# Hybrid retention and sliding-window layer: one chain of retention steps for all heads, the second value pair moved to the front, and a bias table stored from 128 partitions

## The chip, the cores and the metric

The kernel runs on one core of a Trainium2 chip. The core has a matrix engine (TensorE; PE in the profile), a vector engine (VectorE, DVE), a scalar engine (ScalarE, ACT), a general engine (GpSimd, POOL) and SyncE (SP), which here only issues transfers between the on-chip memory and HBM. Each engine works through its own instructions strictly in order. The metric is device time in microseconds (us); lower is better.

## The reference

One step of a one-layer encoder for 1024 prompt tokens and 64 sample tokens (1088 columns in all, T in the code), model width 1024:

```python
rq, rk, rv, rg, sq, sk, sv, ga, gb = split(rms_norm(x, g_attn) @ w_in)
q, k = rope(rq), rope(rk) / 16                      # 4 heads of width 256; v = rv
s = (q @ k.T) * decay ; o = s @ v + (q @ state) * q_dec       # per chunk and head
state = state * gamma**C + (k * k_dec).T @ v                  # handed to the next chunk
a = (rms_norm(o) * silu(rg)) @ w_ret_out
b = attend(sq, band(sk), band(sv), bias_table, sinks) @ w_swa_out   # 16 heads of width 64
x = x + (sigmoid(ga) * a + sigmoid(gb) * b) @ w_mix_out
x = x + cross_attention(rms_norm(x), memory)
x = x + (silu(rms_norm(x) @ w_gate) * (rms_norm(x) @ w_up)) @ w_down
y = rms_norm(x)
```

The 64 sample tokens start from a given retention state and given caches. Outputs are y, the retention states, the last keys and values of the window, and the keys and values of the memory.

## The kernel before

Every fp32 operand of the large products is split into a high and a low part (`split`: a cast on ScalarE, the rest on VectorE, L125 and L126), and each product is made of three matmuls (high·high, high·low, low·high). The stage that the change touches is the first, `project_phase` (L612), which takes about the first 700 us.

**Pairs and products.** The columns of `w_in` are taken in pairs of 128-column tiles (256 columns). A pair is one 2x2 Strassen multiplication (`strassen`, L265): seven products named P1 to P7, each of 24 matmuls on TensorE (L209, L210, L212; four blocks of six). For a pair the weights are loaded (`raw`), summed on GpSimd (L186 to L193) and split into `wq`. The right-hand operands B11 to B22 and T1 to T4 are made once from x at the start (`start_phase`). A product lies in one of three PSUM bank pairs (`pq`) until VectorE or ScalarE has read it (L270, L644).

**What follows a pair.** `rotated` (keys and queries, L663) applies the rotary angles with eight VectorE products and four sums for each pair; the sums are on VectorE for heads 0 and 1 and on GpSimd for heads 2 and 3. `values` (L687) only stores. `queries` (L693) orders the window queries and stores them from GpSimd's queue into `d_sq`. Keys, queries and values of the retention go to a scratch tensor in HBM, `d_qkv`. `stage` is the ring of eight buffers that all of these write.

**The first pair** (values of head 0) is done plainly with eight products (`plain`, L233), while the Strassen operands are still being made. The weights of the second pair are prepared inside `start_phase` on VectorE.

**Retention as side steps.** The retention of a head (`retention`, L827) is a Python generator. It loads four blocks of 256 tokens in turn and the 64 sample tokens last. Each `yield` ends a step: after every Strassen product one step is emitted into TensorE's order (`product`, L215), so that its VectorE and ScalarE work has the next product to hide behind. A block has five steps: transposes of keys and values (`pk`, L823), an empty one, scores (`pss`), the state's update with the transposes of the block's earlier output (`pkv`, `pb` L982), output (`po`). The sample tokens add four (`pk`, `psss`, `pb`, then `pos` and `pkvs`), with the first load one, so 25 steps for a head. `finish_side` (L775) emits whatever steps are left without products between them.

**Sum of squares.** `token_squares` (L505) adds up x squared for the norm, with 14 sums on VectorE (L516); `token_roots` (L518) reduces them over the partitions on TensorE (`pt`, L525) and takes the roots, and `spread_roots` (L530) spreads them again (`pb`, L536). Retention needs them.

**Bias table.** `bias_table` (L584) makes the relative-position bias with one matmul, 16 heads by 256 distances, copies it to `rb` and stores it 64 times over into `d_rb` (1 MB) with one transfer from GpSimd's queue (L597). `bias_rows` (L606) reads it back skewed into `d_bias`.

**Order.** Pairs run k0, q0, k1, q1, v1, window queries 0, k2, q2, v2, window queries 1, k3, q3, v3, window queries 2, window keys/values, window queries 3, gates. Between them a list scheduler, led by priorities and its own timing model, decides the order within each engine; TensorE's order of products and steps is fixed by the code (`in_order`, L1024).

Of the kernel before, what the change touches and what calls it, by code (L numbers as in the profile page):

```python
# [11 lines left out]
F32 = mybir.dt.float32  # L12
# [7 lines left out]
P = 128  # L20
# [7 lines left out]
BLK = 256  # L28
NBLK = SEQ // BLK
H = 4  # L30
# [80 lines left out]
class Kernel:  # L111
# [310 lines left out]
    def start_phase(self, ctx):  # L422

        nc, tc, io = self.nc, self.tc, self.io
# [53 lines left out]
                if k == 2 and n < 2:  # L478
                    weight(1, n)
        with tc.issue_after(behind[0]), tc.issue_after(behind[1]):  # L480
            self.second = self.weight_ops(self.load_raws([io["w_k"][i] for i in range(2)]), by=nc.vector)
            for k in range(4):
                b11, b12 = qs[k][:2]
                for b in (b11, b12):
                    nc.scalar.mul(b, b, g[:, k:k + 1])
                nc.vector.tensor_tensor(out=b12, in0=b12, in1=b11, op=ALU.subtract)
# [97 lines left out]
    def bias_table(self):  # L584

        nc, io = self.nc, self.io
        t = self.ra.tile([P, BLK + 16], F32, tag="sf", bufs=1, name="table")
        rb = self.ra.tile([P, 2, BLK], F32, tag="ot", bufs=1, name="rb")[:16]
        table, onehot = t[:32, BLK:], t[:32, :BLK]
        self.load(table, io["rel_bias"])  # L590
        self.load(onehot, io["c_onehot"])
        pb = self.norm_psum("pb")
        nc.tensor.matmul(pb[:16, :256], table, onehot, start=True, stop=True)
        for i in range(2):
            nc.vector.tensor_copy(rb[:, i, :], pb[:16, :256])
        rb = rb.rearrange("h i c -> h (i c)")
        nc.gpsimd.dma_start(self.d_rb.rearrange("h (i c) -> h i c", c=512), rb.unsqueeze(1).broadcast_to([16, 32, 512]))  # L597
        row = self.np.tile([1, 16], F32, tag="row", bufs=1, name="row")
        self.load(row, io["sinks"])
        ps = self.norm_psum("ps")  # L600
        nc.tensor.matmul(ps[:, :16], self.ones[:1, :], row, start=True, stop=True)
        for e in range(2):
            rows = slice(e * 64, (e + 1) * 64)
            nc.vector.tensor_copy(self.sinks[rows, :], ps[rows, :16].rearrange("p (a b) -> p a b", b=2)[:, :, e])
# [7 lines left out]
    def project_phase(self):  # L612
        nc, tc, io = self.nc, self.tc, self.io
        with ExitStack() as ctx:
# [5 lines left out]
            first = self.start_phase(sctx)  # L620
# [66 lines left out]
            def values(w, h, by=self.strassen):  # L687
                def emit(i, t, ps, sb):
                    self.store(self.d_qkv[2, 2 * h + i, :, half(t)], taken(ps, sb))
                by(w, self.ops, emit)  # L690

            pair = lambda w, h: self.load_ops([io[w][2 * h + i] for i in range(2)])
# [30 lines left out]
            first = self.second  # L723
            sctx.close()
            stage, long, count = *self.stage_tiles(), [0]
            with ExitStack() as rctx:
                self.ra = rctx.enter_context(tc.tile_pool(name="ra", bufs=1, reuse_waits="tile"))
                rope = self.ra.tile([P, 2, T], F32, name="rope")
                self.load(rope, io["c_rope"])
                self.out = None  # L730
                rotated(first, 0, 1)
                with tc.issue_after(self.sums_done):
                    self.token_squares()
                self.side = self.retention_begin()
                rotated(pair("w_q", 0), 0, 0)
                for h in range(1, H):
                    rotated(pair("w_k", h), h, 1)
                    if h == 1:
                        self.finish_side()
                        self.side = self.retention_steps(0)  # L740
                    rotated(pair("w_q", h), h, 0)
                    values(pair("w_v", h), h)
                    queries(pair("w_sq", h - 1), h - 1)
                    self.finish_side()
                    self.side = self.retention_steps(h)
                project(self.load_ops((io["w_sk"], io["w_sv"])), lambda i, t, o: nc.gpsimd.dma_start(self.d_skv[i, :, half(t)], o))
                with tc.issue_after(self.last_sum):
                    self.bias_rows()
                queries(pair("w_sq", 3), 3)
                for m in (0, 2, 4):  # L750
                    gate_columns(1, "w_ga", AF.Sigmoid, m)
                self.finish_side()
# [24 lines left out]
            pass  # L777
        self.side = None

    def retention_begin(self):  # L780
        for i in range(6):
            yield
        self.token_roots()
        self.retention_setup()
        for i in range(3):
            yield
        self.spread_roots()
        yield

    def retention_steps(self, h):  # L790
        yield from self.retention(h)
        if h == 1:
            yield
            self.bias_table()
        if h == H - 1:
            for i in range(3):
                yield
            self.ret_turn(*self.out)

    def retention_setup(self):  # L800

# [1077 lines left out]
```

## Time and profile before

| | |
|---|---|
| median of 3 runs | 2258.58 us (2257.07 to 2261.13) |
| the profiled execution | 2261.93 us, span 2260.1 us |
| TensorE busy | 2171.1 us, 96% of the span |
| VectorE, ScalarE, GpSimd busy | 1596.2, 879.3, 702.6 us |
| granted TensorE clock, mean | 0.984 |

In a row of a timeline the columns are start (us from the span's start), duration, engine, source line, operation, output<-input by the names in the program, shape, and in brackets the engine's idle time just ahead of the row and what ended it. A row of a window table gives the stretch, its length, the busy time of each engine with the number of instructions in brackets, the granted TensorE clock, the busy share of the transfer engines, and GB/s. In a table of waits stand the waiting engine and line, what it waited for, the sum in us, the number of times and the longest. Transfers have sizes in KB and the median time from issue to landing.

### The profile page before, as it was taken

The numbers are of one execution on the slowest core, as the hardware profiler recorded it, in microseconds if no ns is written. First come the engines' busy times: TensorE is split into PE (matmuls) and PEld (weight loads), VectorE is DVE, ScalarE is ACT, GpSimd is POOL, SyncE is SP. The second block draws the span as 40 slices with busy tenths as digits, with TensorE's granted clock in tenths as the row PEclk, the third lists the DMA queues.
The fourth block names the chain that finished last, engine by engine and source line by source line (L and its number), as shares of the span: only waits on it lengthen the run. The fifth ranks groups of instructions, "written<-read, shape, count | busy, mean of one in ns | idle before, by whom it ended". The sixth has DMA issues, their size and how long they took to land.

```text
span 2260.1 us, 42145 instructions
## 1 busy us (share of the span) xinstructions
PE 2171.1 (96%) x16620; PEld 2117.7 (94%) x16620; DVE 1596.2 (71%) x2696; ACT 879.3 (39%) x1895; POOL 702.6 (31%) x522
## 2 busy tenths in 40 slices
PE   9699998999999998999999999999999999999987
PEld 8698998999999996888999999999999999999987
DVE  7886676867668657876544556668777776879787
ACT  6334332435444346554233334333322322335333
POOL 0123234354246111230000000004555555534571
PEclk9799999999999999999999999999999999999999
DMA  5334344443444557325543212332333223376332
GB/s 210 124 104 137 102 129 100 128 133 112 164 140 154 163 202 240 123 77 183 149 141 104 82 39 66 120 105 83 101 131 122 93 101 116 113 246 209 120 120 80
DMA packets 160455, 291.90 MB, mean 129 GB/s; under 512 B 21538, under 2 KB 89058, under 8 KB 160130
## 3 DMA queue, kind: packets, MB, share of 16 engines
q1 hardware_dynamic: 151122, 263.97, 36.0%
q0 software_dynamic: 5104, 17.44, 2.5%
q10 hardware_dynamic: 4032, 7.80, 0.9%
q8 instruction: 131, 2.15, 0.4%
q14 instruction: 66, 0.54, 0.1%
HBM read 197.99 MB, written 91.95 MB: 128 GB/s over the span
## 4 chain that ended last, share of the span: by engine, by line
PE 73%; DVE 12%; DMA 5%; issue 4%; ACT 3%; POOL 3%; SPq 0%; POOLq 0%; DVEq 0%; ACTq 0%
PE pq L209 14%; PE pq L212 14%; PE pq L210 14%; PE pd L152 7%; PE pd L153 7%; PE pd L154 7%; DVE wq L126 2%; DMA hl<-d_op 1%; DVE T L126 1%; PE pss L1103 1%; DVE B L126 1%; PE pout L1169 1%; DVE stage L644 1%; DVE u L270 1%; PE pp L1146 1%
## 5 line engine op out<-in xcount | busy, mean ns | idle before, releaser
L126 DVE TENSOR_TENSOR wq<-raw,wq 128x512 fp32r<-128x512 f32 (+1 forms) x505 | 460.1, 916 | 164.3 <-ACT wq L125 162.2
L125 ACT CAST wq<-raw 128x512 fp32r<-128x512 f32 (+1 forms) x505 | 305.6, 613 | 608.2 <-PE pq L212 255.7
L209 PE MATMUL pq<-T,wq 128*128 128x272 f32 x1832 | 505.5, 294 | 15.5 <-DVE stage L644 5.7
L210 PE MATMUL pq<-T,wq 128*128 128x272 f32 x1832 | 500.0, 289 | 0.6 <-DVE T L126 0.6
L209 PE MATMUL pq<-B,wq 128*128 128x272 f32 x1526 | 419.9, 293 | 0.7 <-DVE stage L644 0.6
L210 PE MATMUL pq<-B,wq 128*128 128x272 f32 x1526 | 415.7, 289 | 0.6 <-DVE B L126 0.5
L212 PE MATMUL pq<-T,wq 128*128 128x272 f32 x1832 | 380.7, 289 | 2.4 <-DVE wq L126 2.4
L186 POOL TENSOR_TENSOR raw<-raw 128x512 f32<-128x512 f32 (+1 forms) x58 | 78.7, 1357 | 962.5 <-DVE rs_r L309 486.0
L209 PEld LDWEIGHTS pq<-T,wq 128*128 128x128 f32 x1832 | 347.7, 190 | 18.6 <-issue 6.9
L210 PEld LDWEIGHTS pq<-T,wq 128*128 128x128 f32 x1832 | 351.3, 192 | 1.1 <-DVE T L126 1.1
L212 PE MATMUL pq<-B,wq 128*128 128x272 f32 x1526 | 317.0, 288 | 0.0
L210 PEld LDWEIGHTS pq<-B,wq 128*128 128x128 f32 x1526 | 291.9, 191 | 1.0 <-DVE B L126 1.0
L209 PEld LDWEIGHTS pq<-B,wq 128*128 128x128 f32 x1526 | 289.0, 189 | 1.8 <-DVE stage L644 0.9
L212 PEld LDWEIGHTS pq<-T,wq 128*128 128x128 f32 x1832 | 286.3, 189 | 2.7 <-DVE wq L126 2.6
L212 PEld LDWEIGHTS pq<-B,wq 128*128 128x128 f32 x1526 | 238.2, 189 | 0.0
L270 DVE TENSOR_TENSOR u<-pq,u 128x544 f32<-128x544 f32 x177 | 127.1, 718 | 87.0 <-PE pq L212 86.5
L189 POOL TENSOR_TENSOR raw<-raw 128x512 f32<-128x512 f32 (+1 forms) x58 | 82.7, 1426 | 122.1 <-DVE wq L126 122.1
L644 DVE TENSOR_TENSOR stage<-pq,u 128x544 f32<-128x544 f32 x112 | 80.1, 716 | 42.5 <-PE pq L212 31.0
L193 POOL TENSOR_TENSOR raw<-raw 128x512 f32<-128x512 f32 (+1 forms) x58 | 88.5, 1527 | 15.7 <-DVE wq L126 12.2
L1131 POOL TENSOR_TENSOR t<-t,den 128x768 f32<-128x768 f32 (+2 forms) x34 | 47.7, 1402 | 137.7 <-DVE nm L1119 53.0
L187 POOL TENSOR_TENSOR raw<-raw 128x512 f32<-128x512 f32 (+1 forms) x58 | 85.3, 1471 | 3.7
L1661 POOL TENSOR_TENSOR y<-u,y 128x544 f32<-128x544 f32 x38 | 61.4, 1632 | 49.6 <-DVE y L1659 29.2
(403 smaller groups left out, 4748.7 us busy)
## 6 DMA issues: line engine op xcount, KB each, us to landing
hl<-d_op SPq DMA_DIRECT2D x84, 272.0 KB, 4.0
d_op<-stage SPq DMA_DIRECT2D x44, 272.0 KB, 2.2
d_op<-ht SPq DMA_DIRECT2D x44, 272.0 KB, 3.9
raw<-w_gate SPq DMA_DIRECT2D x22, 512.0 KB, 3.6
raw<-w_up SPq DMA_DIRECT2D x22, 512.0 KB, 4.6
raw<-w_down SPq DMA_DIRECT2D x16, 512.0 KB, 3.8
d_qkv<-stage SPq DMA_DIRECT2D x28, 272.0 KB, 2.5
d_gate<-stage ACTq DMA_DIRECT2D x28, 272.0 KB, 2.1
```

The lines of the kernel that those rows point to most:

```text
L125: self.last_cast = self.nc.scalar.copy(hi, src).ins
L126: self.last_low = self.nc.vector.tensor_tensor(out=lo, in0=src, in1=hi.bitcast(F32), op=ALU.subtract).ins
L152: mm(ps, wh, xh, start=start, stop=False)
L153: mm(ps, wh, xl, start=False, stop=False)
L154: self.last_mm = mm(ps, wl, xh, start=False, stop=stop).ins
L187: tt(out=a21, in0=a21, in1=a22, op=add)
L193: self.last_sum = tt(out=a12, in0=a12, in1=a11, op=sub).ins
L209: mm(ps[:, c, :HC], w[:, 0, ks], x[:, 0, cs], start=start, stop=False)
L210: mm(ps[:, c, :HC], w[:, 0, ks], x[:, 1, cs], start=False, stop=False)
L212: self.last_mm = mm(ps[:, c, :HC], w[:, 1, ks], x[:, 0, c * HC:(c + 1) * HC], start=False, stop=stop).ins
L270: add = lambda out, a, b: nc.vector.tensor_tensor(out=out, in0=a, in1=b, op=ALU.add)
L644: nc.vector.tensor_tensor(out=o, in0=ps, in1=sb, op=ALU.add)
```

## The change

Four things are done.

1. The second pair, prepared in `start_phase`, is the values of head 1 instead of the keys of head 0. The keys of head 0 become the third pair, with weights prepared by GpSimd as for the others. Values of head 1 no longer stand between q1 and window queries 0.
2. The four generators of the heads, and the one for the roots ahead of them, become a single one, `retention_steps`. It starts after q0 (before: the roots with q0, head 0 with q1), and it is finished once, after the third gate pair. No head's remaining steps are emitted at the end of a pair group. In all 112 products carry its steps.
3. Within the chain the roots are three steps in, the spreading three steps later, and the bias table stands right behind head 1.
4. The bias matmul's weights are widened by a VectorE copy from 16 columns to 128, each head eight times over. The result lies on 128 partitions, and each stores four of the 32 repetitions that before 16 partitions stored.

```diff
@@ start_phase
-            self.second = self.weight_ops(self.load_raws([io["w_k"][i] for i in range(2)]), by=nc.vector)
+            self.second = self.weight_ops(self.load_raws([io["w_v"][2 + i] for i in range(2)]), by=nc.vector)
@@ bias_table
-        rb = self.ra.tile([P, 2, BLK], F32, tag="ot", bufs=1, name="rb")[:16]
+        rb = self.ra.tile([P, 2, BLK], F32, tag="ot", bufs=1, name="rb")
+        wide = self.ra.tile([P, P], F32, tag="qsm", bufs=1, name="wide")[:32]
...
-        nc.tensor.matmul(pb[:16, :256], table, onehot, start=True, stop=True)
+        nc.vector.tensor_copy(wide.rearrange("p (h r) -> p h r", r=8), table.unsqueeze(2).broadcast_to([32, 16, 8]))
+        nc.tensor.matmul(pb[:, :256], wide, onehot, start=True, stop=True)
         for i in range(2):
-            nc.vector.tensor_copy(rb[:, i, :], pb[:16, :256])
+            nc.vector.tensor_copy(rb[:, i, :], pb[:, :256])
         rb = rb.rearrange("h i c -> h (i c)")
-        nc.gpsimd.dma_start(self.d_rb.rearrange("h (i c) -> h i c", c=512), rb.unsqueeze(1).broadcast_to([16, 32, 512]))
+        nc.gpsimd.dma_start(self.d_rb.rearrange("h (r i c) -> (h r) i c", r=8, c=512), rb.unsqueeze(1).broadcast_to([P, 4, 512]))
@@ project_phase
-                rotated(first, 0, 1)
+                values(first, 1)
+                rotated(pair("w_k", 0), 0, 1)
                 with tc.issue_after(self.sums_done):
                     self.token_squares()
-                self.side = self.retention_begin()
                 rotated(pair("w_q", 0), 0, 0)
+                self.side = self.retention_steps()
                 for h in range(1, H):
                     rotated(pair("w_k", h), h, 1)
-                    if h == 1:
-                        self.finish_side()
-                        self.side = self.retention_steps(0)
                     rotated(pair("w_q", h), h, 0)
-                    values(pair("w_v", h), h)
+                    if h > 1:
+                        values(pair("w_v", h), h)
                     queries(pair("w_sq", h - 1), h - 1)
-                    self.finish_side()
-                    self.side = self.retention_steps(h)
@@ the generators
-    def retention_begin(self):
-        for i in range(6):
+    def retention_steps(self):
+        for i in range(3):
             yield
         self.token_roots()
         self.retention_setup()
...
         self.spread_roots()
         yield
-
-    def retention_steps(self, h):
-        yield from self.retention(h)
-        if h == 1:
+        for h in range(H):
+            yield from self.retention(h)
+            if h == 1:
+                self.bias_table()
+                yield
+        for i in range(3):
             yield
-            self.bias_table()
-        if h == H - 1:
-            for i in range(3):
-                yield
-            self.ret_turn(*self.out)
+        self.ret_turn(*self.out)
```

VectorE, ahead of the roots (`pt` is read by L307). Before, the last sums of squares stand among the rotation of q0 (L675 to L681), right ahead of the roots:

```order
L516 TENSOR_TENSOR rstd<-rstd,xsq 128x544
L678 TENSOR_TENSOR stage_523<-stage_523,rope 128x544
L680 TENSOR_TENSOR stage_522<-stage_522,stage_523 128x544 x2
L516 TENSOR_TENSOR rstd<-rstd,xsq 128x544
L681 TENSOR_TENSOR stage_523<-stage_523 128x544
L307 TENSOR_SCALAR rs_v<-pt 128x8
```

Now the last sum of squares stands in the middle of the pair k0 (u_751 belongs to k0's P7):

```order
L516 TENSOR_TENSOR rstd<-rstd,xsq 128x544
L270 TENSOR_TENSOR u_752<-pq,u_750 128x544
L126 TENSOR_TENSOR wq<-raw,wq 128x512
L516 TENSOR_TENSOR rstd<-rstd,xsq 128x544
L270 TENSOR_TENSOR u_751<-pq,u_750 128x544
L646 TENSOR_TENSOR stage_523<-pq,u_752 128x544
```

The roots' L307 follows 54 rows after the last L516, where before it was two rows after it. On TensorE `pt` stands 11 products later: before it is behind the 22nd product of the program, now behind the 33rd.

TensorE, the sample tokens of head 0. Before, the four steps stand without a product between them:

```order
L154 MATMUL po<-vb,ss 128x256
L823 MATMUL pk<-ident,vf 64x128 x4
L938 MATMUL psss<-qsm,vf 64x64 x2
L982 MATMUL pb<-ident,ret_o 128x128 x4
L947 MATMUL pos<-state,qsm 64x256 x2
L948 MATMUL pos<-kvs,sfs 64x256
L951 MATMUL pkvs<-kvs 128x256 x2
L209 MATMUL pq<-B_173,wq 128x272
```

Now there are 24 matmuls of a product on each side of a step; around the third row (`psss`):

```order
L210 MATMUL pq<-B_178,wq 128x272
L212 MATMUL pq<-B_178,wq 128x272 x2
L935 MATMUL psss<-qsm,vf 64x64 x2
L209 MATMUL pq<-T_181,wq 128x272
L210 MATMUL pq<-T_181,wq 128x272
```

All four steps of head 0 are moved in this way, as they stood already for heads 1 to 3.

GpSimd, the store of the bias table. Before, it stands between the products of window queries 1 and directly ahead of their two pairs of stores:

```order
L193 TENSOR_TENSOR raw<-raw 128x512
L597 DMA d_rb<-rb 512x1x512
L711 DMA d_sq<-stage_522 128x1024
L712 DMA d_sq<-stage_522 128x2x32
L705 TENSOR_TENSOR stage_522<-stage_523,rstd 128x8x64
L707 TENSOR_TENSOR stage_522<-stage_523,rstd 128x32
L711 DMA d_sq<-stage_522 128x1024
```

Now it stands behind the stores of k3 and ahead of the weight sums of another pair, and the next transfer of this queue is six rows on:

```order
L686 DMA d_qkv<-stage_523 128x544
L599 DMA d_rb<-rb 512x1x512
L186 TENSOR_TENSOR raw<-raw 128x512
L187 TENSOR_TENSOR raw<-raw 128x512
L189 TENSOR_TENSOR raw<-raw 128x512
L193 TENSOR_TENSOR raw<-raw 128x512
L683 TENSOR_TENSOR stage_522<-stage_522 128x544
L686 DMA d_qkv<-stage_522 128x544
```

On TensorE the bias matmul is now behind product 87 of the program instead of 77, one product after head 1's last step instead of two.

## The prediction

> **What bounds the kernel now.** I read the page first, then TensorE's waits in the first 700 us (the projection stage, the only one whose code changes), then the timelines around each long wait.
>
> ```profile
> PE 2171.1 (96%) x16620; PEld 2117.7 (94%) x16620; DVE 1596.2 (71%) x2696; ACT 879.3 (39%) x1895; POOL 702.6 (31%) x522
> ```
> ```profile
> PE pt L525 <- DVE rstd L516: 12.8, 1, 12.8
> PE pb L982 <- DVE sf L886: 7.3, 1, 7.3
> ...
> PE pss L152 <- DVE kt L860: 6.2, 6, 1.9
> ...
> PE pb L982 <- ACT ret_o L972: 4.3, 1, 4.3
> ```
>
> TensorE is busy for 96% of the span, so the kernel gets shorter where TensorE stands still or runs slowly, and nowhere else: the change keeps the products, the retention matmuls and their number. Three of these rows are single long waits: for the sums of squares, for VectorE at head 2's first block, and in head 0's sample tokens. The change works on each of the three places.
>
> **The change, term by term.** A, the wait for the squares:
>
> ```profile
> 89.48 0.95 PE L525 MATMUL pt<-ones,rstd 128*128 128x2 f32 x8
> 103.20 2.17 PE L525 MATMUL pt<-ones,rstd 128*128 128x2 f32 x10 [12.77 <-DVE rstd L516]
> 105.30 0.59 PE L209 MATMUL pq<-B,wq 128*128 128x272 f32 x1
> ...
> 110.78 0.29 PE L209 MATMUL pq<-B,wq 128*128 128x272 f32 x1
> ...
> 113.79 0.29 PE L209 MATMUL pq<-T,wq 128*128 128x272 f32 x1
> ```
>
> TensorE reaches the roots behind q0 and stands for 12.77 us. What comes next is slow as well: from 105.30 to 113.79 lie two products, eight blocks of six matmuls. The last four blocks take 113.79 - 110.78 = 3.01 us, which is also the time of a full product at full speed; the first four take 5.48. That is 2.5 us more, and the second part of the roots (2.1 us for 10 rows, where 0.95 us went for 8) adds some 0.8. A = 12.8 + 2.5 + 0.8 = 16.1 us.
>
> ```profile
> 62.05 1.97 DVE L644 TENSOR_TENSOR stage<-pq,u 128x544 f32<-128x544 f32 x3
> ...
> 102.44 0.71 DVE L516 TENSOR_TENSOR rstd<-rstd,xsq 128x544 f32<-128x544 f32 x1
> 103.07 0.71 DVE L681 TENSOR_TENSOR stage<-stage 128x544 f32<-128x544 f32 x1
> ```
> ```profile
> 67.48 0.29 PE L209 MATMUL pq<-B,wq 128*128 128x272 f32 x1
> ```
>
> VectorE is late because two rotated pairs and the squares meet: 57 operations by the order from 62.05 to 103.78, 0.73 us each. With the unrotated v1 second, the last square is some 25 operations into this stretch (about 62 + 18 = 80 us, where its data allows it), and `pt` comes 11 products = 33 us later than TensorE's 89.5. This wait should go entirely. Is VectorE then late for something else? Up to the end of q0 the order now has 72 operations, at 0.73 us 52.6, so until about 114.7. TensorE began the third pair at 67.48 and needs 14 products of 3.01 us for k0 and q0, so it ends q0 at about 109.6. But VectorE's last operations there are q0's rotation, for which TensorE does not wait, and three bank pairs let TensorE run ahead. I charge 1.5 us, with bounds 0 and 5.1 (the whole lag of 114.7 - 109.6).
>
> B, head 0's sample tokens, beside those of head 1, which had products between them:
>
> ```profile
> 219.76 0.38 PE L823 MATMUL pk<-ident,vf 128*64 128x128 f32 x2
> ...
> 231.26 0.39 PE L209 MATMUL pq<-B,wq 128*128 128x272 f32 x1
> ```
> ```profile
> 329.20 0.60 PE L823 MATMUL pk<-ident,vf 128*64 128x128 f32 x4
> 332.75 0.45 PE L938 MATMUL psss<-qsm,vf 128*64 128x64 f32 x4
> 336.25 0.60 PE L982 MATMUL pb<-ident,ret_o 128*128 128x128 f32 x4
> 339.80 1.08 PE L947 MATMUL pos<-state,qsm 128*64 128x256 f32 x4
> ...
> 342.44 0.39 PE L209 MATMUL pq<-T,wq 128*128 128x272 f32 x1
> ```
>
> Head 0 takes 231.26 - 219.76 = 11.5 us. For head 1 the distances less one product of 3.01 us are 0.54, 0.49 and 0.54, and the last step takes 2.64: together 4.2 us. The chain gives head 0 the same form, so B = 7.3 us.
>
> C, the bias table's store:
>
> ```profile
> d_rb<-rb POOLq DMA_DIRECT2D x1, 1024.0 KB, 13.1
> d_sq<-stage POOLq DMA_DIRECT2D x2, 512.0 KB, 10.6
> raw<-w_q SPq DMA_DIRECT2D x2, 512.0 KB, 12.7
> ```
> ```profile
> 366.79 0.58 POOL L711 DMA_DIRECT2D d_sq<-stage  x1 [9.44 <-issue]
> ```
> ```profile
> 371.70 0.69 DVE L126 TENSOR_TENSOR wq<-raw,wq 128x512 fp32r<-128x512 f32 x1 [8.23 <-ACT wq L125]
> 374.36 0.72 DVE L644 TENSOR_TENSOR stage<-pq,u 128x544 f32<-128x544 f32 x1 [1.96 <-DMA d_sq<-stage]
> ```
> ```profile
> 378.94 0.44 PE L982 MATMUL pb<-ident,ret_o 64*128 64x64 f32 x2 [7.35 <-DVE sf L886]
> 379.31 0.59 PE L209 MATMUL pq<-B,wq 128*128 128x272 f32 x1
> ...
> 383.56 0.34 PE L209 MATMUL pq<-B,wq 128*128 128x272 f32 x1
> ```
>
> The 1 MB store takes 13.1 us, 80 GB/s. In these 50 us the weights of q2 take 12.7 us and the `d_sq` stores 10.6; GpSimd's queue stands 9.44 us ahead of its next store, VectorE waits for those weights and then for a stage buffer, and TensorE, whose row names VectorE's `sf`, stands for 7.35 us. The three blocks from 379.31 to 383.56 take 4.25 us instead of 2.26. C = 7.35 + 2.0 = 9.4 us.
>
> ```profile
> swin<-d_sq SPq DMA_DIRECT2D x4, 1024.0 KB, 5.3
> ...
> d_sq<-stage POOLq DMA_DIRECT2D x8, 512.0 KB, 4.3
> ```
>
> The store from 128 partitions does not occur yet. Nearest are a load of the same size to 128 partitions, 5.3 us, and stores of half the size from the same queue, 4.3 (double: 8.6). Bounds 5.3 and 13.1; I take 6, as the size is the same. At its new place GpSimd's queue has only weight sums behind it. I leave 0.5 us of C as lost. [...]
>
> D, small waits of the steps:
>
> ```profile
> 266.75 0.36 PE L152 MATMUL pss<-qs,ks 128*128 128x256 f32 x1 [1.92 <-DVE kt L860]
> ...
> 268.73 0.43 PE L209 MATMUL pq<-T,wq 128*128 128x272 f32 x1
> ...
> 270.09 0.43 PE L209 MATMUL pq<-T,wq 128*128 128x272 f32 x1
> ```
>
> These are the six waits of 6.2 us above. They can cost more than they last: behind the 1.92 us a block takes 1.36 us (270.09 - 268.73) instead of 0.75, and two to three such blocks add some 1.4 us. They occur where a block of retention falls on VectorE's rotation:
>
> ```profile
> 250.00:260.00 10.00, 10.00 (x81) 9.80 (x81) 10.00 (x14) 3.73 (x10) 4.71 (x3) 1.00 0.05 11
> ...
> 320.00:330.00 10.00, 10.00 (x83) 9.99 (x83) 3.95 (x8) 2.05 (x6) 0.53 (x1) 1.00 0.51 166
> ```
>
> VectorE is full in the first stretch (the pairs k2, q2) and 40% busy in the second (v2). The blocks now fall elsewhere: q2 and q3 meet the light sample tokens and the bias table, k2 and k3 still meet full blocks, and heads follow each other without the products that had no step. The work is the same, so I set D to 0, with bounds +9 (all these waits and two slow stretches gone: 6.2 + 2.8) and -9 (twice as many). [...]
>
> What else moves is covered. The weights of v1 are as large as those of k0 and are prepared by the same code. Its four stores stand in SP's queue ahead of later loads of x for the squares, for which 33 us are there. The widening copy and its wait sit on VectorE one product ahead of the matmul that reads it; uncovered it is one operation under 0.5 us.
>
> ```profile
> 600.41 0.36 SPq L122 DMA_DIRECT2D d_ret<-ret_t  x1
> 601.25 0.35 SPq L119 DMA_DIRECT2D raw<-w_ga  x1
> ```
>
> The chain's end comes six products (18 us) later against the products. Behind its last store SP's queue holds the next pair's weights: before those of the fourth gate pair, six products ahead of their use; now those of the first w_rg pair, with seven. If they came late, TensorE would stand about 3 us there.
>
> Sum: 16.1 + 7.3 + 9.4 = 32.8, less 1.5 and 0.5: 30.8 us. The profiled execution would go from 2261.93 us (span 2260.1) to 2231.1; the median of the runs shown lies 3.35 us below it, so 2227.8, said as **2228 us**. TensorE stays at over 95% to the end, so later stages give nothing of it back.
>
> **Rivals.**
> 1. The store still blocks (the widening doesn't do what it says): 13.1 us is due to 64 repeated 2 KB pieces or to GpSimd's queue, not to 16 partitions. For it: GpSimd's own 9.44 us. Against: the 8 stores of the same queue with 4.3 us. The other place may hide it, so half to all of C is lost: 2233 to 2237.
> 2. VectorE becomes the bound in the early pairs: the squares' wait returns as waits for bank pairs. For it: 72 operations until 114.7 us. Against: the last of them are the rotation. With the full 5.1 us and a slow stretch of 2.5, so 6.1 more than charged: 2234.
> 3. Slower than before: the chain without pauses lets VectorE fall behind in every block, and TensorE waits at each `pss` as it did at 266.75, with 1.9 + 1.4 = 3.3 us. In 16 blocks that is 53 us, less the 9 already there 44, more than the gain: 2272. From ten more such blocks on (33 us) the change does not pay. For it: VectorE at 10.00 of 10 us in the rotated pairs. Against: head 1's steps had the same density, one a product, with waits in few blocks, and VectorE has room in the value and window pairs.
> 4. D goes the other way: small waits vanish, and the clock stays up: 2219.
>
> **How the numbers follow.** The forecast with its own range 2220 to 2236 has 0.60, rival 1 0.12, rival 2 0.12, rival 4 0.09, and rival 3 0.07, of which 0.04 end above the time before and 0.03 near it. The range that should hold 8 in 10 is 2214 to 2243: the three terms with D at +9 and nothing lost (2216.8) and 2 to 3 for what I don't see, up to rivals 1 and 2 together (2227.8 + 8.9 + 6.1). The noise of this measurement is about 0.2%, 4.5 us; the three runs spread over 4.1. All cases but rival 3 are below 2254: faster 0.93, same 0.03, slower 0.04.
>
> **What would show it.** The wait of L525 for L516 is gone from TensorE's waits (A); head 0's `pk`, `psss`, `pb`, `pos` stand 3.5 us apart (B); `d_rb` lands in 4 to 9 us and no wait of 7 us stands at head 2's first `pb` (C); the `pss` waits sum to 0 to 15 us (D). Wrong it would be with a new wait over 3 us: for bank pairs between 66 and 115 us (rival 2), at most `pss` steps (rival 3), or behind the chain's end.

## The result, and the profile after

The changed kernel takes 2232.35 us (median of four runs, 2230.57 to 2237.74), the kernel before beside it 2259.27 us (2257.07 to 2261.13). The ratio is 0.9885 with a 95% interval of 0.9866 to 0.9905, a gain of 26.9 us by the medians. A second comparison of the same two gave 2236.18 against 2262.29 us, 0.9887 (0.9873 to 0.9901). The forecast was 30.8 us less and 2228 us.

The profiled execution was the slowest of its four, 2237.74 us with a span of 2235.7. Its busy row, and TensorE's waits from 80 to 700 us (engine and line, who released it: sum in us, count, longest):

```profile
PE 2166.8 (97%) x16620; PEld 2117.3 (95%) x16620; DVE 1605.8 (72%) x2697; ACT 881.7 (39%) x1897; POOL 703.6 (31%) x522
```
```profile
PE po L152 <- DVE state L899: 3.3, 2, 2.4
PE pb L536 <- ACT rstd L538: 3.2, 1, 3.2
PE pss L152 <- DVE kt L857: 2.5, 1, 2.5
PE psss L935 <- DVE kvs L929: 2.3, 1, 2.3
PE pq L209 <- DVE stage L646: 2.1, 2, 1.6
PE pb L979 <- ACT ret_o L969: 2.0, 1, 2.0
...
```

The two large rows of before, 12.8 us for the squares and 7.3 us for `sf`, are gone, and so is the 4.3 us in head 0's sample tokens. No new wait is as long as these. But six waits of 1.6 to 3.2 us stand here, and the longest, for `rstd` of line 538, is one that the prediction did not name.

To see where the time went I cut the projection stage at the same marks in both traces and took from each piece what its products and steps need at full speed. The differences, after less before, in the profiled executions:

| piece | forecast | profiles |
|---|---|---|
| start, up to the first product | 0 | +1.0 |
| A, roots' wait for the squares | -16.1 | -16.3 |
| waits for bank pairs up to the roots | +1.5 | +2.5 |
| the spread of the roots | 0 | +4.9 |
| B, head 0's sample tokens | -7.3 | -7.3 |
| C, around head 2's first block | -8.9 | -9.5 |
| D, all small waits of the steps with their slow matmuls | 0 | +1.8 |
| behind the stage | 0 | -1.4 |
| sum | -30.8 | -24.3 |

The spans differ by 24.4 us. The three terms for which the change was counted came to 33.1 instead of 32.3 us; what was missed lies mostly in the spread and in D, which had been set to 0. A second profiled execution of the changed kernel is 4.3 us shorter in this stage (667.1 against 671.4 us), so a piece of one or two us in this table can be chance.

Three timelines of TensorE in the changed kernel, for B, for the spread, and for head 2's first `pb`, where C's stall had been (start, duration, engine, line, operands; in brackets the wait ahead and its releaser):

```profile
236.73 0.60 PE L820 MATMUL pk<-ident,vf 128*64 128x128 f32 x4
...
240.28 0.45 PE L935 MATMUL psss<-qsm,vf 128*64 128x64 f32 x4
...
243.79 0.60 PE L979 MATMUL pb<-ident,ret_o 128*128 128x128 f32 x4
...
247.34 1.08 PE L944 MATMUL pos<-state,qsm 128*64 128x256 f32 x4
...
249.97 0.39 PE L209 MATMUL pq<-T,wq 128*128 128x272 f32 x1
```
```profile
138.74 0.39 PE L536 MATMUL pb<-ident,rtok 128*128 128x128 f32 x2
142.29 0.43 PE L536 MATMUL pb<-ident,rtok 64*128 64x64 f32 x2 [3.17 <-ACT rstd L538]
```
```profile
382.20 0.33 PE L979 MATMUL pb<-ident,ret_o 64*128 64x64 f32 x2
```

Head 0's steps stand 3.55, 3.51 and 3.55 us apart and the last takes 2.63, as head 1's did before. Head 2's first `pb` has no wait. The spread is the new wait: its third piece needs a bank of a pool with two, and the first piece's copy has not run. ScalarE and GpSimd show why:

```profile
140.62 1.14 ACT L125 CAST wq<-raw 128x512 fp32r<-128x512 f32 x2 [5.30 <-POOL raw L189]
141.66 1.31 ACT L538 COPY rstd<-pb 128x512 f32<-128x512 f32 x3
```
```profile
138.90 1.68 POOL L189 TENSOR_TENSOR raw<-raw 128x512 f32<-128x512 f32 x1 [7.05 <-DVE wq L126]
```
```profile
138.04 0.18 DVE L809 SCALAR_TENSOR_TENSOR tok<-tok 128x36 f32<-128x36 f32 x1
138.14 0.68 DVE L126 TENSOR_TENSOR wq<-raw,wq 128x512 fp32r<-128x512 f32 x1
```

The copies of line 538 stand behind two weight casts in ScalarE's order. These wait for a weight sum on GpSimd, which waits for a difference on VectorE, and VectorE makes that only behind the roots' own small operations. In the kernel before, TensorE has no wait at the spread.

The bias table's store, from the views of DMA issues around 350 to 470 us, in the changed kernel:

```profile
d_rb<-rb POOLq DMA_DIRECT2D x1, 1024.0 KB, 6.9
```

It lands after 6.9 us where 13.1 us stood, and no wait of GpSimd's queue for the issue follows it.

### The profile page after: what moved, and what is told of

It is laid out like the page before. It is cut to its first block, busy times and chain, and to the rows that moved or that the text cites. A ratio compares the mean times of both kernels' runs of the same rounds, so it can differ in the third digit from the quotient of the medians.

```text
span 2235.7 us, 42154 instructions
## 1 busy us (share of the span) xinstructions
PE 2166.8 (97%) x16620; PEld 2117.3 (95%) x16620; DVE 1605.8 (72%) x2697; ACT 881.7 (39%) x1897; POOL 703.6 (31%) x522
## 4 chain that ended last, share of the span: by engine, by line
PE 74%; DVE 10%; DMA 6%; POOL 3%; issue 3%; ACT 3%; SPq 0%; DVEq 0%; ACTq 0%; POOLq 0%
PE pq L209 14%; PE pq L212 14%; PE pq L210 13%; PE pd L152 7%; PE pd L153 7%; PE pd L154 7%; DVE wq L126 3%; PE pss L1100 1%; DVE T L126 1%; DMA hl<-d_op 1%; DVE B L126 1%; DMA xsq<-xT 1%; PE pout L1166 1%; ACT wq L125 1%; POOL raw L189 1%
## 5 line engine op out<-in xcount | busy, mean ns | idle before, releaser
L193 POOL TENSOR_TENSOR raw<-raw 128x512 f32<-128x512 f32 (+1 forms) x58 | 85.6, 1476 | 16.1 <-DVE wq L126 12.5
```

The lines of the kernel that those rows point to most:

```text
L193: self.last_sum = tt(out=a12, in0=a12, in1=a11, op=sub).ins
```

## The experiments

Each was timed in turns with the kernel before on the same chip, so ratios to that kernel are compared, and within a set the times too. The kernel before had a median of 2259.27 us beside the change's first row, 2261.48 in the first set of experiments (the narrow store to the burst), 2262.26 in the second (the spread to the two edits together) and 2262.29 in the third (the change's second row and the last three).

| kernel | median us | ratio to before | 95% interval |
|---|---|---|---|
| the change, first time | 2232.35 | 0.9885 | 0.9866 to 0.9905 |
| the change, third set | 2236.18 | 0.9887 | 0.9873 to 0.9901 |
| narrow store at the new place | 2236.97 | 0.9890 | 0.9873 to 0.9907 |
| before, wide store alone | 2252.25 | 0.9953 | 0.9939 to 0.9966 |
| key pair second | 2233.58 | 0.9870 | 0.9854 to 0.9887 |
| head 0's last steps in a burst | 2242.35 | 0.9904 | 0.9887 to 0.9922 |
| spread in three steps | 2234.27 | 0.9872 | 0.9854 to 0.9890 |
| bias transfers later | 2233.32 | 0.9871 | 0.9853 to 0.9889 |
| stage buffers by return | 2226.94 | 0.9844 | 0.9827 to 0.9860 |
| stage buffers and spread | 2221.97 | 0.9821 | 0.9803 to 0.9838 |
| these two and bias transfers later | 2222.72 | 0.9825 | 0.9812 to 0.9839 |
| these three, key pair second | 2232.20 | 0.9868 | 0.9854 to 0.9881 |
| before, single chain alone | 2238.69 | 0.9889 | 0.9873 to 0.9906 |

**The store: its width, and its place.** Two kernels take the fourth part of the change apart. In the first, the changed kernel stores the table from 16 partitions again:

```diff
-        rb = self.ra.tile([P, 2, BLK], F32, tag="ot", bufs=1, name="rb")
-        wide = self.ra.tile([P, P], F32, tag="qsm", bufs=1, name="wide")[:32]
+        rb = self.ra.tile([P, 2, BLK], F32, tag="ot", bufs=1, name="rb")[:16]
...
-        nc.gpsimd.dma_start(self.d_rb.rearrange("h (r i c) -> (h r) i c", r=8, c=512), rb.unsqueeze(1).broadcast_to([P, 4, 512]))
+        nc.gpsimd.dma_start(self.d_rb.rearrange("h (i c) -> h i c", c=512), rb.unsqueeze(1).broadcast_to([16, 32, 512]))
```

> The changed kernel with the bias table stored from 16 partitions again, at its new place in the chain. Theory (the 16 partitions make the store long, and the long store is what blocks): d_rb takes about 13 us again instead of 6.9, GpSimd's next transfer stands behind it, and a part of the old stall returns around 370 to 400 us: 3 to 9 us, so 2235 to 2241 us. Rival (the other place in the chain is what removed the stall): d_rb takes 13 us too, but no wait over 1 us is new there, and the time stays within 2 us of 2232.

In the second, the kernel before gets the wide store, by the same lines the other way round, and nothing else:

> The kernel before with the bias table stored from 128 partitions, everything else as it was. Theory (the length of the store blocks): d_rb falls from 13.1 to about 7 us, GpSimd's wait of 9.44 us ahead of d_sq to about 3, the 7.35 us at head 2's first pb goes, and the time falls by 8 to 9.5, to about 2250 us. Rival (the place blocks, whatever the length): more than half of the stall stays, 2254 to 2259 us.

The first came to 2236.97 us, ratio 0.9890, which cannot be told from the changed kernel's. Its store is long again, and TensorE hardly notices (DMA issues, then TensorE at head 2's first block):

```profile
d_rb<-rb POOLq DMA_DIRECT2D x1, 1024.0 KB, 12.4
```
```profile
379.13 0.31 PE L977 MATMUL pb<-ident,ret_o 64*128 64x64 f32 x2 [0.41 <-DVE sf L881]
```

The second came to 2252.25 us, 0.9953 (0.9939 to 0.9966): the wide store alone is worth 7.7 to 13.8 us at its old place. Its DMA issues, GpSimd's queue and TensorE at the old place of the stall:

```profile
d_rb<-rb POOLq DMA_DIRECT2D x1, 1024.0 KB, 4.7
...
raw<-w_q SPq DMA_DIRECT2D x2, 512.0 KB, 6.0
```
```profile
359.21 0.58 POOL L713 DMA_DIRECT2D d_sq<-stage  x1 [1.02 <-issue]
```
```profile
372.63 0.31 PE L984 MATMUL pb<-ident,ret_o 64*128 64x64 f32 x2 [0.30 <-DVE sf L888]
```

With the store at 4.7 us the next store of GpSimd's queue waits 1.02 us to be issued instead of 9.44, the weights of q2 come after 6.0 us instead of 12.7, and TensorE's 7.35 us shrink to 0.30. So the prediction's chain of causes holds at the old place. At the new place even 12.4 us do little harm. In these two kernels either half of the move removes the stall (in the chain alone, the last kernel below, 2.7 us of it are left); the sum C was right, and it would have been right with the narrow store too, nearly.

**The squares: v1 second, or roots later.** The changed kernel with the first key pair second again:

```diff
-            self.second = self.weight_ops(self.load_raws([io["w_v"][2 + i] for i in range(2)]), by=nc.vector)
+            self.second = self.weight_ops(self.load_raws([io["w_k"][i] for i in range(2)]), by=nc.vector)
...
-                values(first, 1)
-                rotated(pair("w_k", 0), 0, 1)
+                rotated(first, 0, 1)
...
-                    if h > 1:
-                        values(pair("w_v", h), h)
+                    values(pair("w_v", h), h)
```

> The changed kernel with the first key pair second again and the second value pair behind the first window of queries of head 1, so the long chain alone, with the roots three products behind q0. Theory (the squares are late because two rotated pairs meet them): the last square stands at about 104 us as before, TensorE reaches the roots at about 98.5, so a wait of 5 to 6 us stays and some 2 us of slow matmuls behind it: 2239 us, 6 to 8 over the changed kernel. Rival (the later place of the roots removes the wait by itself): no wait over 1 us at the roots, 2230 to 2234 us.

It took 2233.58 us, 0.9870 (0.9854 to 0.9887): no slower than the change. VectorE's last sum of squares, and TensorE at the roots and at their spread:

```profile
102.66 0.72 DVE L516 TENSOR_TENSOR rstd<-rstd,xsq 128x544 f32<-128x544 f32 x1
```
```profile
103.43 0.72 PE L525 MATMUL pt<-ones,rstd 128*128 128x2 f32 x5 [1.40 <-DVE rstd L516]
...
117.27 3.11 PE L536 MATMUL pb<-ident,rtok 128*128 128x128 f32 x18 [1.81 <-DVE rtok L312]
```

The squares are as late as before the change, 102.66 us, as I expected. But TensorE waits 1.40 us, not 5 to 6. I had put the roots three products later than before, and it is four: three pauses, and the roots behind the next product. Four products are 12.0 us, nearly the whole of the 12.77. In the changed kernel the last sums start at 86.42 us, the roots come seven products later than here, and nothing waits. The later place of the roots thus removes most of A by itself, but not all: behind each of the two waits TensorE's clock is at 0.50 for 3.41 us (from 105.06 and from 118.71 us), which by an estimate from the halved clock costs 1.7 us each, so 6 to 7 of the 16.1 us stay. The changed kernel loses as much in the same part of its profile, 4.9 us at the spread and 2.5 us for bank pairs, which is why the times do not differ. The value pair takes away the last 1.4 and 1.8 us and moves the spread to a place where it can wait for ScalarE instead. With the other edits the order is worth something, as the last but one kernel below shows.

**The burst.** In the changed kernel head 0's last four steps are put back together, with three products without a step behind them:

```diff
-            self.in_order(self.step)
+            while self.in_order(self.step) == "on":
+                pass
...
-            yield from self.retention(h)
+            for i, x in enumerate(self.retention(h)):
+                yield "on" if h == 0 and i in (21, 22, 23) else None
+            if h == 0:
+                for i in range(3):
+                    yield
```

> The changed kernel in which head 0's last four steps (keys and values, scores, turn, output of the sample tokens) stand without a product between them, and three products without a step follow, so that all later steps keep their products. Theory (the products between hide the latency of these steps): the four steps take about 11.5 us instead of 4.2, and the time rises by 7.3 to 2239.5 us. Rival (the burst gives the other engines a rest that later steps use): VectorE and ACT come out of it ahead, later small waits shrink, and the rise is under 4 us.

It took 2242.35 us, 0.9904 (0.9887 to 0.9922), 4 us over the change by the ratios, whose intervals overlap. The trace is sharper than the times:

```profile
233.87 0.60 PE L825 MATMUL pk<-ident,vf 128*64 128x128 f32 x4
236.67 0.45 PE L940 MATMUL psss<-qsm,vf 128*64 128x64 f32 x4 [2.20 <-DVE kvs L934]
238.67 0.84 PE L984 MATMUL pb<-ident,ret_o 128*128 128x128 f32 x4 [1.55 <-ACT ret_o L974]
239.44 1.83 PE L949 MATMUL pos<-state,qsm 128*64 128x256 f32 x4
...
242.24 2.07 PE L953 MATMUL pkvs<-kvs 64*128 64x256 f32 x4
244.24 0.59 PE L209 MATMUL pq<-B,wq 128*128 128x272 f32 x1
```

The steps take 244.24 - 233.87 = 10.4 us instead of 4.2, the last at about half speed, and the products behind them lose another 2.6 us to slow matmuls. From the first product to the stage's last mark this execution is 679.2 us long, the changed kernel's 671.4: 7.8 us, where the prediction had 7.3. This difference is uncertain by some 4 us, as the second execution of the changed kernel took 667.1; the steps and the slow matmuls by themselves give 6.2 + 2.6 = 8.8 us. The rival's rest for the other engines does not show in the trace: TensorE's waits behind the burst sum to 8.7 us, and to 9.4 in the changed kernel from 250 us on. The times alone would not decide between the two.

**The spread.** Now the wait that I had not seen. The spread in three steps, and the roots two products earlier so that head 0 begins where it did:

```diff
     def retention_steps(self):
-        for i in range(3):
+        for i in range(1):
             yield
...
-        self.spread_roots()
-        yield
+        yield from self.spread_roots()
@@ spread_roots
             self.nc.scalar.copy(self.rstd[:, c0:c0 + n], pb[:, :n])
+            yield
```

> The changed kernel with the roots two products earlier and the spread of the roots in three steps, one matmul chunk and one copy each, so that head 0 begins at the same product as now. Theory (the third chunk waits for a bank whose copy stands on ScalarE behind weight casts, and a product between the chunks covers it): the wait of 3.17 us for rstd and the 1.6 us of slow matmuls behind it go, 2227 to 2228 us. Rival (ScalarE is held by the weight sums in any case): the wait moves to a later chunk or to the next step, and the time stays at 2231 to 2233 us.

It took 2234.27 us, 0.9872 (0.9854 to 0.9890). The wait is gone from TensorE's list, but part of it comes back one step on. The largest row of that list, from 80 to 700 us:

```profile
PE pss L152 <- DVE kt L857: 4.0, 2, 2.4
```

One of the two is head 0's first `pss`, which now waits 1.5 us and did not wait before this edit. The ratio is 3 us below that of the change, with intervals that overlap, so the times do not settle it, and there is a reason beside the noise. Kernels with the same order at that place showed this wait at 3.17, 3.33, 1.94, 0.69 and 0.40 us. The change run again was there to see whether the edits elsewhere caused that:

> The changed kernel again, unedited, beside the three others of this set. Theory: 2231 to 2236 us as before, with the wait of the spread of the roots for rstd anywhere from 0.4 to 3.3 us, since kernels with the same order there showed 0.40, 0.69, 1.94, 3.17 and 3.33 us. Rival: 3 us are what this order costs, and the smaller values belong to the edits elsewhere.

It showed 2.02 us, where the first execution of the same kernel had 3.17. So the size of the wait varies with the execution, by 1.15 us in this pair; whether 0.40 and 0.69 us belong to the same scatter or to the edits of those kernels is not shown. The 4.9 us in the table above are near the upper end of what was seen.

**The stage buffers.** VectorE's waits for a stage buffer (line 646, the sum that empties a bank pair), changed kernel, 80 to 600 us:

```profile
DVE stage L646 <- DMA d_sq<-stage: 9.9, 2, 5.4
DVE stage L646 <- DMA d_qkv<-stage: 9.6, 5, 3.4
```

and the two of these that stand ahead of TensorE's waits of 2.46 and 2.32 us:

```profile
396.33 0.72 DVE L646 TENSOR_TENSOR stage<-pq,u 128x544 f32<-128x544 f32 x1 [3.45 <-DMA d_qkv<-stage]
...
460.70 0.72 DVE L646 TENSOR_TENSOR stage<-pq,u 128x544 f32<-128x544 f32 x1 [5.44 <-DMA d_sq<-stage]
```

VectorE stands for a store that still reads its buffer, and the retention's operations queue behind it. There were two readings. Either the queue is too slow there, since the two bias transfers of `bias_rows` lie on it ahead of the `d_sq` stores; or the eight buffers go round in a circle in which the first buffer of a pair is the one that the pair before stored last. The first was tried by issuing the bias transfers behind the last window queries:

```diff
-                with tc.issue_after(self.last_sum):
-                    self.bias_rows()
                 queries(pair("w_sq", 3), 3)
+                with tc.issue_after(self.last_sum):
+                    self.bias_rows()
```

> The changed kernel with the two bias transfers (d_bias) issued behind the last window queries instead of ahead of them. Theory (the bias transfers on GpSimd's queue are what delays the stores of d_sq at 452 us): VectorE's wait of 5.44 us for d_sq and TensorE's 2.32 us at head 2's psss go, 2229 to 2230 us. Rival (the stage buffer is asked for again too soon, whatever lies on the queue): VectorE still waits 3 to 4.5 us for d_sq there, as it does at 517 us where no bias transfer is near, TensorE keeps 1 us or more, and the time stays within 1.5 us of 2232.

The second by handing the buffers out in the order in which they were given back, temporaries of the rotation first (the long rows of the window queries are two neighbours from the same list):

```diff
-                count[0] += 1
-                return stage[(count[0] - 1) % len(stage)]
+                held.append(free.pop(0))
+                return stage[held[-1]]
...
+                    free.extend((held.pop(), held.pop(), at[0, t], at[1, t]))
```

> The changed kernel with the eight stage buffers handed out in the order in which they were given back (temporaries of the rotation and the early half of the stores first) instead of round in a fixed circle. Theory (VectorE's waits for a stage buffer that a store still reads are what makes TensorE wait at 104.89, 399.22, 465.18 and 520.20 us): these four waits go with the slow matmuls behind them, 8 to 10 us, 2222 to 2224 us. Rival (VectorE is late there because of its own work and of the weight sums): the waits get other releasers and keep more than half of their length, 2228 to 2232 us.

Bias transfers later: 2233.32 us, 0.9871 (0.9853 to 0.9889). The wait at `psss` is gone from TensorE's list and `d_sq` lands after 3.5 us there instead of 6.1, so for this one place the first theory holds, though the time cannot be told from the change's. The others stay: 1.8 us at the `pss` of 399 us, 2.2 us at the `po` of 520.

Buffers by return: 2226.94 us, 0.9844 (0.9827 to 0.9860). TensorE's list from 80 to 700 us; the row left out at its end has 0.3 us:

```profile
PE pb L536 <- ACT rstd L538: 1.9, 1, 1.9
PE pb L985 <- ACT ret_o L975: 1.9, 1, 1.9
PE pq L209 <- DVE stage L646: 1.3, 3, 0.5
PE po L152 <- DVE state L905: 0.5, 1, 0.5
PE pss L152 <- DVE kt L863: 0.4, 1, 0.4
...
```

The waits at 104.89, 399.22, 465.18 and 520.20 us are gone or under 0.5 us, and VectorE's line 646 no longer waits for any store. From the first product to the stage's end it is 661.5 us against 671.4 and 667.1 in the two profiled executions of the change: 6 to 10 us. The queue explains one of these waits, the circle explains all.

**Both edits together.** The spread in three steps and the buffers by return together:

> The changed kernel with both: the spread in three steps with earlier roots, and the stage buffers in the order of their return. Theory (the two waits are independent): the gains add to 12 to 15 us, 2217 to 2220 us. Rival (they share VectorE as their cause): the sum is 3 us or more below that, 2222 to 2225 us.

It took 2221.97 us, 0.9821 (0.9803 to 0.9838), and its interval lies below that of the change. From the stage's first product to its end it takes 657.0 us. The sum of 12 to 15 us is what came out by the ratios (0.9821 against 0.9885 and 0.9887 is 14 to 15 us); the median itself lies above the 2217 to 2220 us expected, with a kernel before that was 3 us slower in this set than beside the change's first row. Adding the later bias transfers:

> The kernel with the stage buffers in the order of their return and the spread in three steps, and with the two bias transfers behind the last window queries as well. Theory (moving the bias transfers helped only because a stage buffer was asked for while its store was late, and with the buffers in the new order nobody asks): no further change, within 3 us of the kernel without it, 2219 to 2225 us. Rival (the transfers also hold GpSimd's sums and the loads of weights): 3 us or more faster.

2222.72 us, 0.9825: nothing more, as expected. Beside the change in the same set this is 13.5 us less. The last piece, v1's place, was put to the test once more in this kernel:

> The same kernel with all three edits, and with the first key pair second again, the second value pair behind head 1's window queries. Theory (with the stage waits gone only the roots differ): the roots wait about 1.4 us for the squares, the spread about 1.8 us for the roots, with the slow matmuls behind them 4 to 6 us more than with the value pair second: 2224 to 2228 us. Rival (the earlier start of head 0 gives the chain six products more at its end and later steps meet lighter pairs, as the few waits of this order showed): no slower than with the value pair second, 2217 to 2222 us.

2232.20 us, 0.9868 (0.9854 to 0.9881): 9.5 us slower, more than either side had.

```profile
105.52 2.17 PE L525 MATMUL pt<-ones,rstd 128*128 128x2 f32 x10 [7.62 <-DVE rstd L516]
```

I had overlooked that this kernel's roots stand two products earlier than those of the kernel with the key pair second above. The wait is 7.62 us where it was 1.40, so 6.2 us more: counted from each kernel's first product, TensorE reaches the roots 4.3 us earlier and the last sum of squares comes 1.9 us later. So the two means against the squares' wait can stand in for each other. Whoever wants the roots early needs the value pair second; with the roots two products later it brings nothing that these runs can measure.

**The chain alone.** In the kernel before, the second and third parts of the change only (the key pair stays second, by the diff above, and the store narrow):

> The kernel before with one part of the change alone: the single chain behind the first queries. The first key pair stays second and the bias table is stored from 16 partitions. Theory (the chain's later roots, its spacing of the sample tokens and its place for the store each remove their stall, the other two parts only secure it): 2232 to 2238 us, nearly all of the gain; d_rb takes 12 to 13 us and no wait over 2 us for VectorE's sf is left at head 2's first pb. Rival (the parts need each other): the long store stalls TensorE again by 5 us or more and the squares' wait adds to it, 2240 us or more.

2238.69 us, 0.9889 (0.9873 to 0.9906): the same ratio as the whole change, within an interval of some 4 us to each side (the five runs lie between 2231 and 2242 us). Some of what the other parts secure shows in TensorE's waits:

```profile
PE pb L975 <- DVE sf L879: 4.8, 3, 2.7
...
PE pb L536 <- DVE rtok L312: 1.9, 1, 1.9
PE pt L525 <- DVE rstd L516: 1.6, 1, 1.6
```

The store takes 12.5 us here, and 2.7 us of wait stand for `sf` at head 2's first `pb`, a little over the 2 us I had allowed; with 3.41 us at half clock behind it this costs an estimated 4.4 us, not far from the rival's 5. Of the four parts, the chain carries the gain, as far as these times can tell.

## Why the prediction was right or wrong

**The time and the sign were right**, the gain 4 us too large: 30.8 us forecast, 26.9 and 26.1 us by the medians of two comparisons, and at most 30.3 us by the lower end of the first interval.

**A** was right in size (16.3 us in the profiles against 16.1) and half right in cause. The prediction put the lateness down to two rotated pairs that meet the squares. With the pairs meeting as before but the roots four products later, a wait of 1.40 us remained, and with the wait at the spread and the slow matmuls 6 to 7 us. The step "this wait should go entirely" named two reasons; the later roots alone do more than half.

**VectorE's lag, charged at 1.5 us,** measured 2.5 in the profile with its slow matmuls, and the reason was another. VectorE was not late through its 72 operations; one wait of 2.22 us for a `d_qkv` store stood ahead of TensorE's 1.64:

```profile
104.02 0.72 DVE L646 TENSOR_TENSOR stage<-pq,u 128x544 f32<-128x544 f32 x1 [2.22 <-DMA d_qkv<-stage]
```

With the buffers in the order of return the row for bank pairs fell from 2.1 to 1.3 us.

**B** was right: 7.3 us, and 7.8 us when it was put back (uncertain by some 4 us).

**C** was right in size (9.5 against 8.9) and its chain of causes was shown at the old place. The size of the wide store, taken as 6 us, was 4.7 to 8.1 us in the eleven profiled executions that have it, with a median of 6.4. What the prediction gave to rival 1 as "the other place may hide it" is the case: the place would have hidden even a store that still took 12.4 us.

**D, set to 0,** came to +1.8 us in the profile, well inside its bounds of 9. "The work is the same" was the failing sentence here. The waits were not a matter of how much work VectorE has but of which buffer it is given: about 10 us of the change's stage hung on that, and the prediction's own row of VectorE waiting 1.96 us for a `d_sq` store already showed it. The size of +1.8 us is in part chance: the waits that are left are fewer and longer than before, and whether one is followed by slow matmuls differs with where it falls (1.99 and 2.32 us in the last section).

**"What else moves is covered" failed.** The spread of the roots was moved to a new place and was not listed. I named what is queued behind moved transfers, but not what is queued on ScalarE ahead of the copies that free the spread's two banks. It cost 4.9 us in one profiled execution, and waits of 0.4 to 3.3 us in six with the same order. Its 3.17 us are over the 3 us that the prediction gave as a sign of being wrong, at a place that it had not named. With D it makes up the 6.4 us between the forecast and the profiled executions, the other pieces nearly cancelling; by the medians 3.9 and 4.7 us are missing.

**Rivals.** Rival 1 did not occur: the width does shorten the store (12.4 to 13.1 us from 16 partitions, 4.7 to 8.1 from 128). Rival 2's 6 us did not come. Rival 3 was wrong: one step a product without pauses has no wait at most blocks, since only one `pss` wait is left. Rival 4, the small waits gone, did not occur with the change. In the kernel of both edits they are mostly gone (one of 2.0 us and one of 1.0 are the longest left), but that took other means; that its 2222 us lie near the 2219 of this rival says nothing for the rival.

## What to carry to other kernels

When a step is moved, list the engine that frees its buffers and what stands ahead of that operation in its order, not only the step's own matmuls and transfers. Where an engine waits for a buffer whose store has not landed, look at which buffer it was handed before looking at the bandwidth: giving them out in the order of their return was worth 9 to 10 us here by the ratios, while the wide store brought nothing measurable at its new place. Two means against one stall hid each other here, at the squares and at the store, so a gain is shared out only after each has been tried alone.

## What the runs showed of the hardware that I had not expected

**The width of a store counted, and the wide store's time varied.** From issue to landing, 1 MB from 16 partitions took 13.1, 12.4 and 12.5 us, 80 to 85 GB/s, and from 128 partitions 4.7 to 8.1 us, 129 to 223 GB/s. At the old place it was 13.1 against 4.7 us, at the new one 12.4 against 6.9. Between executions that store the same bytes from the same 128 partitions the time thus differed by a factor of 1.7.

**TensorE's granted clock changed in stretches of 3.41 us, and of two waits the shorter was followed by half clock.** Two waits of TensorE in the changed kernel, each with the window table of the stretches around it (the granted clock is the third number from the end):

```profile
351.33 1.09 PE L979 MATMUL pb<-ident,ret_o 128*128 128x128 f32 x4 [1.99 <-ACT ret_o L969]
```
```profile
348.24:351.65 3.41, 1.42 (x11) 1.08 (x10) 3.41 (x7) 1.50 (x4) 1.97 (x3) 1.00 0.22 71
351.65:355.07 3.42, 3.42 (x17) 3.34 (x16) 3.38 (x7) 0.54 (x2) 3.42 (x2) 0.50 0.10 37
355.07:358.48 3.41, 3.41 (x20) 2.32 (x19) 2.81 (x2) 1.27 (x3) 3.39 (x4) 1.00 0.46 165
```
```profile
465.18 0.45 PE L935 MATMUL psss<-qsm,vf 128*64 128x64 f32 x4 [2.32 <-DVE kvs L929]
```
```profile
460.88:464.29 3.41, 1.98 (x16) 1.76 (x14) 2.97 (x9) 1.02 (x3) 1.94 (x2) 1.00 0.78 249
464.29:467.70 3.41, 2.52 (x21) 2.45 (x22) 3.41 (x8) 1.64 (x4) 0.89 (x1) 1.00 0.49 150
```

Behind the shorter wait the clock is 0.50 for one stretch, behind the longer one it stays at 1.00. In each of the fourteen traces the granted clock changes only at times that lie whole multiples of 3.41 us apart, and these times differ between executions (93.53, 110.59 and 223.23 us in the kernel before, 143.44, 351.65 and 399.44 us in the changed one). The wait of 1.99 us falls into one such stretch. The wait of 2.32 us is cut by the edge at 464.29 us into 1.43 and 0.89 us.

Counted over the fourteen traces, from 75 to 700 us: a stretch at full clock in which TensorE stood idle for 1.89 us or more was followed by half clock in all 28 cases (in the kernel before 1.92 us from 264.20, in the changed one 1.99 us from 348.24 and 2.46 us from 396.03). Of the stretches with at most 1.77 us of idle time only six were, and all six hold matmuls of the roots, which are two columns wide; from 1.78 to 1.83 us both occur (1.83 us from 370.01 in the kernel before was followed by full clock). What a stretch at half clock costs a steady run of products is an estimate: 1.7 us by the halved clock, 1.5 by the block of six matmuls that took 1.36 us instead of 0.75 behind the wait at 266.75 us in the kernel before. So the same waits can cost different times: they sum to 15.6 and 15.2 us in the two profiled executions of the changed kernel, but the first has three stretches at half clock in the stage behind 80 us and the second has one, which by the estimate would be 3.0 to 3.4 of the 4.3 us between them.

No run varied the idle time of a stretch alone, and what part the roots' narrow matmuls and the transposes have in the clock was not separated here.
